# Two layer norms of a decoder trunk: gain and shift applied behind the transposition, as per-partition scalars

## The chip, the core and the metric

The kernel runs on one core of one Trainium2 chip. The metric is the device time of one execution in microseconds (us). PE is the matrix engine, DVE the vector engine, ACT the scalar engine, POOL is GpSimd, SP the engine whose queue issues nearly all DMAs.

## The reference, cut to what matters

```python
def layer_norm(x, g, b):
    xf = x.astype(jnp.float32)
    mu = jnp.mean(xf, -1, keepdims=True)
    var = jnp.mean(jnp.square(xf - mu), -1, keepdims=True)
    return ((xf - mu) * lax.rsqrt(var + LN_EPS) * g + b).astype(x.dtype)

x = layer_norm(x, ln_in_g, ln_in_b)
memn = layer_norm(mem, ln_mem_g, ln_mem_b)
for l in range(DEPTH):
    h = x @ w_in[l]
    ...                                  # two attention groups on slices of h
    x = layer_norm(DEEPNORM_ALPHA * x + mix, ln1_g[l], ln1_b[l])
    xa = memory_cross_attn(x, memn, xa_wq[l], xa_wkv[l], xa_wo[l])
    x = layer_norm(DEEPNORM_ALPHA * x + xa, ln2_g[l], ln2_b[l])
    f = conv_ffn(x, w_up, conv_w, conv_b, w_down)
    x = layer_norm(DEEPNORM_ALPHA * x + f, ln3_g[l], ln3_b[l])
```

x and mem are 256 rows of 1024, all in 32-bit floats; there are two layers. The first norm of x is wanted twice: transposed, for the products with w_in, and in its natural form, for the residual at the end of the first attention block.

## The kernel before

Every large product is taken with split operands: a number is a high part (rounded by ACT, `hi` and `xh`) and a low part (the rest, by a subtraction on DVE, `lo` and `xl`), and three of the four partial products are summed in PSUM. The 256 rows are two tiles of 128 (t = 0, 1), the 1024 columns are 8 chunks of 128 (k = 0 to 7).

Weights stream through `piece` (called by `wmat`): SP loads 512 KB into one of 4 `raw` buffers, ACT makes `hi` (L130), DVE makes `lo` (L131) out of `raw` and `hi`. A `raw` buffer is free when both have read it; the `hi` and `lo` buffers (6 of each) are free when PE has used them. SP issues its loads in a fixed order, so one load that waits for a `raw` buffer holds all behind it. The first pieces are w_kc (2 pieces), then those of the steps nq1, nq0, k (2 each), the compression's w1 (4) and v (3).

The program starts with a few matmuls on ones (`warm`) and with the first norm. Four matmuls of one row of ones (L274) spread gain and shift over 128 partitions in PSUM. `layer_norm` takes the statistics (DVE for t = 0, ACT for t = 1), GpSimd the reciprocal root (L209), and DVE applies mean, gain, root and shift in two passes of two halves (L239, L240). `transposed` then transposes 4 chunks at a time on PE (L247), ACT rounds them into xh (L250), and DVE subtracts into xl (L251). The memory's norm (`mem_norm`) does the same with gain and shift broadcast by DMA (`mg`, 512 KB each).

The steps of a block are named in a list (CFG, 'attn'): kc nq1 nq0 par k cmp v mem tab qk0 ... In `in_kc` (L487) the three partial products come in the order hi·xh, hi·xl, lo·xh. The step tab loads `neg` and lets GpSimd make the bias table alibi, 8 instructions (L323), before the other tables. In `compress` the hidden layer lies in PSUM (cmp); DVE copies it to `hs` (L160), and PE transposes `hs` (L523).

A scheduler gives each engine one fixed order of instructions out of the program, and each engine keeps to it; the row of an instruction is thus also what stands in front of it.

Of the kernel before, what the change touches and what calls it, by code (L numbers as in the profile page):

```python
# [53 lines left out]
def consts():  # L54
# [35 lines left out]
def trunk(ctx: ExitStack, tc: tile.TileContext, a: dict, out: bass.AP):  # L90
# [24 lines left out]
    RAW, HL, PP = SIZES  # L115

    def piece(nk, n, segs, wn=None, cols=None):
        r = wp.tile([P, 1024], F32, name="raw", tag="raw", bufs=RAW)
        rv = r[:, :nk * n].rearrange("p (k n) -> p k n", k=nk)
        for krange, crange, src, *pr in segs:  # L120
            p0, p1 = pr[0] if pr else (0, P)
            nc.sync.dma_start(rv[p0:p1, krange[0]:krange[1], crange[0]:crange[1]], src)
        wn = wn or n
        h = wp.tile([P, 1024], F32R, name="hi", tag="hi", bufs=HL)
        lo = wp.tile([P, 1024], F32R, name="lo", tag="lo", bufs=HL)
        hv = h[:, :nk * wn].rearrange("p (k n) -> p k n", k=nk)
# [53 lines left out]

    xn = [big.tile([P, D], F32, name=f"x{t}", tag=f"x{t}") for t in range(NT)]
    nc.sync.dma_start(xn[0], a["x"][0, 0:P, :])

    def load_gb(g, b, tags=("vmla", "k0")):
        ts_ = []
# [6 lines left out]
    nc.sync.dma_start(xn[1], a["x"][0, P:2 * P, :])
    rows = big.tile([1, 2, D], F32, name="rows", tag="oTh")
    for i, v in enumerate(("ln_in_g", "ln_in_b")):
        nc.scalar.dma_start(rows[:, i], a[v].rearrange("(o d) -> o d", o=1))
    ident = loadc("c_ident", [P, P])
    ones = big.tile([P, 512], F32R, name="ones", tag="q0")
# [10 lines left out]
    def rsqrt(o, x):  # L208
        G.tensor_tensor(o, x, mhalf, op=ALU.pow)  # L209
# [53 lines left out]
    def new_xT():  # L263
# [52 lines left out]
    cok = const.tile([P, NT, HN, 16], F32, name="c_cok", tag="c_cok")  # L316
    alibi = const.tile([P, HN, S], BF16, name="alibi", tag="alibi")

    def load_tables():
        neg = tmp.tile([P, S], F32, name="neg", tag="pT", bufs=4)  # L320
        nc.sync.dma_start(neg, a["c_neg"])
        for h in range(HN):
            G.tensor_scalar(alibi[:, h, :], neg, float(8.0 * 2.0 ** (-(h + 1))), None, op0=ALU.mult)  # L323
        nc.sync.dma_start(tri, a["c_tri"])
        nc.sync.dma_start(cs, a["c_cs"])
        nc.sync.dma_start(kcs, a["c_kcs"])
        nc.sync.dma_start(ctab, a["c_ctab"])
        nc.sync.dma_start(cok, a["c_cok"])
# [2 lines left out]

    def mem_norm():
        mb = big.tile([P, NT, D], F32, name="mb", tag="xkl")
        mg = big.tile([P, 2, D], F32, name="mg", tag="xkh")
        mn, mgb = [mb[:, t] for t in range(NT)], [mg[:, i] for i in range(2)]
        for i, v in enumerate(("ln_mem_g", "ln_mem_b")):
            nc.sync.dma_start(mgb[i], bcast(a[v], D))
# [58 lines left out]
    for l in range(DEPTH):  # L396
# [388 lines left out]
        def mem():  # L785
# [276 lines left out]
```

## Time and profile before

| | us |
|---|---|
| median of 3 runs | 878.4 (877.24 to 880.74) |
| the profiled execution, its own time | 879.98 |
| its span on the core | 877.9 |
| PE busy in the span | 860.3 |
| DVE busy | 665.2 |
| ACT busy | 532.5 |
| GpSimd busy | 132.4 |

Times in the views are counted from the span's start. Each view is one profiled execution. PE's share counts a matmul as busy until its modelled end. A matmul on 256 columns follows the one ahead of it at 0.12 us at the full granted clock.

### The profile page before, as it was taken

What the parts mean: (1) busy time and instruction counts of PE and PEld (TensorE: products, weight loads), DVE (VectorE), ACT (ScalarE), POOL (GpSimd) and SP (SyncE); (2) the same over time, 40 slices, a digit from 0 to 9 for tenths busy, and PEclk for the clock granted to TensorE, in tenths of its full rate; (3) what the DMA queues carried; (4) which work ended last, traced back from release to release, by engine and by line L of the source; (5) the groups of instructions that cost most, each with busy time, mean ns of one, the idle gap of its engine ahead of it and who ended that gap; (6) DMA issues with size and microseconds to landing.
All of it is one profiled execution on the core that took longest, in us unless ns stands there. A gap on an engine that the chain in (4) does not pass through costs nothing.

```text
span 877.9 us, 14948 instructions
## 1 busy us (share of the span) xinstructions
PE 860.3 (98%) x5502; PEld 766.7 (87%) x5502; DVE 665.2 (76%) x1290; ACT 532.5 (61%) x1014; POOL 132.4 (15%) x140
## 2 busy tenths in 40 slices
PE   8989999999999999999999999999999999999996
PEld 5989798899989888888989998879998888888895
DVE  7789887766578877677688788968566877777777
ACT  5658764555546676666555678636573567667661
POOL 1052000000000332222300020000000033223220
PEclk9989999999999999999999999999999999999998
DMA  7944463476347756656538634446633655665641
GB/s 229 284 145 124 132 173 113 140 251 190 96 123 237 217 158 216 190 165 217 183 110 239 190 90 110 144 127 210 194 119 121 218 159 179 212 192 171 215 142 48
DMA packets 128236, 148.66 MB, mean 169 GB/s; under 512 B 6259, under 2 KB 111009, under 8 KB 128163
## 3 DMA queue, kind: packets, MB, share of 16 engines
q1 hardware_dynamic: 128159, 147.70, 54.5%
q8 instruction: 43, 0.70, 0.3%
q14 instruction: 30, 0.25, 0.1%
q10 hardware_dynamic: 4, 0.01, 0.0%
HBM read 146.64 MB, written 1.05 MB: 168 GB/s over the span
## 4 chain that ended last, share of the span: by engine, by line
PE 91%; DVE 4%; ACT 2%; DMA 2%; issue 1%; POOL 0%; SPq 0%; DVEq 0%; ACTq 0%; POOLq 0%
PE up L259 16%; PE up L261 8%; PE acc L996 5%; PE acc L997 5%; PE acc L998 5%; PE acc L170 3%; PE acc L171 3%; PE acc L169 3%; PE fill L178 2%; PE fill L179 2%; PE xq L179 2%; PE xq L178 2%; PE xq L177 2%; PE fill L171 2%; PE fill L169 2%; PE fill L170 2%
## 5 line engine op out<-in xcount | busy, mean ns | idle before, releaser
L131 DVE TENSOR_TENSOR lo<-raw,hi 128x1024 fp32r<-128x1024 f32 (+5 forms) x296 | 322.8, 1108 | 96.2 <-ACT hi L130 94.0
L130 ACT ACTIVATE hi<-raw 128x1024 fp32r<-128x1024 f32 (+5 forms) x296 | 275.8, 951 | 108.9 <-PE acc L171 34.4
L259 PE MATMUL up<-xT,hi 128*128 128x512 f32 x608 | 152.1, 392 | 0.0
L259 PEld LDWEIGHTS up<-xT,hi 128*128 128x128 f32 x608 | 110.3, 189 | 20.3
L261 PEld LDWEIGHTS up<-xT,lo 128*128 128x128 f32 x608 | 82.9, 190 | 5.9
L984 POOL TENSOR_TENSOR cv<-cv 128x256 f32<-128x256 f32 x40 | 54.2, 1356 | 218.7 <-ACT cv L982 170.0
L261 PE MATMUL up<-xT,lo 128*128 128x256 f32 x608 | 84.8, 282 | 0.0
L978 ACT ACTIVATE cv<-u,par 128x256 f32<-128x256 f32 x76 | 45.4, 598 | 49.6 <-DVE u L971 49.6
L996 PE MATMUL acc<-hi,frh 128*128 128x512 f32 x176 | 68.9, 392 | 0.0
L997 PE MATMUL acc<-lo,frh 128*128 128x512 f32 x176 | 68.8, 391 | 0.0
L998 PE MATMUL acc<-hi,frl 128*128 128x512 f32 x176 | 68.2, 389 | 0.0
L209 POOL TENSOR_TENSOR mv<-mv,mhalf 128x1 f32<-128x1 f32 x16 | 14.3, 897 | 309.0 <-DVE mv L233 158.5
L979 DVE SCALAR_TENSOR_TENSOR cv<-u,par,cv 128x255 f32<-128x255 f32 x76 | 37.6, 495 | 26.4 <-ACT cv L978 26.4
L584 ACT ACTIVATE p<-p,nm 128x128 f32<-128x128 f32 x96 | 42.6, 447 | 9.7 <-DVE nm L581 9.4
L986 ACT ACTIVATE frh<-cv 128x256 fp32r<-128x256 f32 x44 | 18.4, 418 | 37.8 <-POOL cv L984 35.4
L987 POOL TENSOR_TENSOR frl<-cv,frh 128x256 fp32r<-128x256 f32 x40 | 38.0, 952 | 20.3 <-ACT frh L986 20.3
L980 DVE SCALAR_TENSOR_TENSOR cv<-u,par,cv 128x254 f32<-128x254 f32 x76 | 37.9, 498 | 2.5
L998 PEld LDWEIGHTS acc<-hi,frl 128*128 128x128 f32 x176 | 33.0, 188 | 7.5 <-DVE frl L987 0.7
L996 PEld LDWEIGHTS acc<-hi,frh 128*128 128x128 f32 x176 | 33.1, 188 | 7.0 <-ACT frh L986 0.9
L997 PEld LDWEIGHTS acc<-lo,frh 128*128 128x128 f32 x176 | 33.1, 188 | 6.0
L177 PE MATMUL fill<-mTh,hi 128*128 128x256 f32 x128 | 37.2, 291 | 0.0
L179 PE MATMUL fill<-mTh,lo 128*128 128x256 f32 x128 | 36.6, 286 | 0.0
(279 smaller groups left out, 2151.7 us busy)
## 6 DMA issues: line engine op xcount, KB each, us to landing
raw<-in_ffn_w_up SPq DMA_DIRECT2D x88, 512.0 KB, 4.4
raw<-in_ffn_w_down SPq DMA_DIRECT2D x44, 512.0 KB, 4.3
raw<-in_xa_wkv SPq DMA_DIRECT2D x32, 512.0 KB, 3.8
raw<-in_xa_wq SPq DMA_DIRECT2D x16, 512.0 KB, 5.4
raw<-in_xa_wo SPq DMA_DIRECT2D x16, 512.0 KB, 4.2
raw<-in_w_in SPq DMA_DIRECT2D x24, 256.0 KB, 3.4
raw<-in_w_out SPq DMA_DIRECT2D x16, 256.0 KB, 4.6
raw<-in_w_out SPq DMA_DIRECT2D x8, 512.0 KB
```

Of the source, the lines that this page charges most:

```text
L130: A.activation(h_, x_, AF.Copy)
L131: V.tensor_tensor(l_, x_, h_.bitcast(F32), op=ALU.subtract)
L169: T.matmul(o, xh_[:, t, k], h, start=k == 0, stop=False)
L177: T.matmul(o, h[:, ms], xh_[:, :, k], start=k == 0, stop=False)
L179: T.matmul(o, lo[:, ms], xh_[:, :, k], start=False, stop=k == len(ws) - 1)
L259: T.matmul(o, h[:, ms], x2[:, k], start=k == 0, stop=False)
L261: T.matmul(o[:, 0:S], lo[:, ms], x2[:, k, 0], start=False, stop=k == len(ws) - 1)
L978: A.activation(c, u, AF.Identity, bias=pcol("cb", l, ft), scale=w_[2])
L984: E.tensor_tensor(conv[0], conv[0], conv[1], op=ALU.mult)
L996: T.matmul(o, fh[:, ts_], h[:, cs_], start=f == 0, stop=False)
L997: T.matmul(o, fh[:, ts_], lo[:, cs_], start=False, stop=False)
L998: T.matmul(o, fl[:, ts_], h[:, cs_], start=False, stop=f == NF - 1)
```

## The change

The broadcast of gain and shift by matmul, and mg with its two broadcast loads, are gone. ACT's queue loads the four vectors as a tile of 32 rows; one transposition makes `gcol`, in which a column holds gain or shift of 128 features. `normalized` takes the statistics on DVE for both tiles and applies mean and root in one pass (L281 of the kernel after). `affine_T` transposes, and then ACT applies gain and shift as scale and bias per partition while it rounds (L293); DVE does the same in two instructions, into y and then xl (L295, L296), one chunk k of both tiles at a time.

The low parts of w_kc are made by GpSimd (`share`; L133), and the table alibi is made by GpSimd from the start on. A new step nx, between par and k, loads gain and shift broadcast (gbx, 2 x 512 KB) and lets GpSimd bring both tiles of x to their natural form in four passes. In `in_kc` the order is hi·xh, lo·xh, hi·xl. In CFG only 'nx' is added.

```diff
+        E = G if share["on"] else V
...
-            V.tensor_tensor(l_, x_, h_.bitcast(F32), op=ALU.subtract)
+            E.tensor_tensor(l_, x_, h_.bitcast(F32), op=ALU.subtract)
...
+    rows = tmp.tile([32, P], F32, name="rows", tag="pT", bufs=4)
+    for i, v in enumerate(("ln_in_g", "ln_in_b", "ln_mem_g", "ln_mem_b")):
+        nc.scalar.dma_start(rows[8 * i:8 * i + 8], a[v].rearrange("(k p) -> k p", p=P))
...
+    def normalized(y):
...
+        for c in range(2):
+            V.bn_stats(s6[:, c, :], y[:, c * 512:(c + 1) * 512])
+        V.bn_aggr(mv[:, 0:2], s6)
+        V.tensor_scalar(mv[:, 2:3], mv[:, 1:2], LN_EPS, None, op0=ALU.add)
+        rsqrt(mv[:, 3:4], mv[:, 2:3])
+        V.tensor_scalar(y, y, mv[:, 0:1], mv[:, 3:4], op0=ALU.subtract, op1=ALU.mult)
+
+    def affine_T(zs, i, h, lo):
...
+                T.transpose(pts[k // 2][:, c0:c0 + P], zs[t][:, k * P:(k + 1) * P], ident)
+        for k in range(KD):
...
+            A.activation(h[:, :, k], src, AF.Identity, scale=g_, bias=b_)
+            y = tmp.tile([P, NT, P], F32, name="y", tag="pp", bufs=PP)
+            V.tensor_scalar(y, src, g_, b_, op0=ALU.mult, op1=ALU.add)
+            V.tensor_tensor(lo[:, :, k], y, h[:, :, k].bitcast(F32), op=ALU.subtract)
...
-    gb = []
-    for i in range(2):
-        gb.append([bank("fill") for _ in range(2)])
-        for c in range(2):
-            T.matmul(gb[i][c], ones[0:1, 0:P].bitcast(F32), rows[:, i, c * 512:(c + 1) * 512], start=True, stop=True)
+    pg = bank("fill")
+    T.transpose(pg[:, 0:32], rows, ident[0:32, 0:32])
+    V.tensor_copy(gcol.rearrange("p a k -> p (a k)"), pg[:, 0:32])
+    warm(12, 512)
     xh, xl = new_xT()
     for t in range(NT):
-        layer_norm(xn[t], gb, act=cfg['lnact']['in'][t])
-        if t:
-            warm(6, 512)
-        transposed(xn[t], t, xh, xl)
-
+        normalized(xn[t])
+    share["on"] = True
     w_kc = wmat(a["w_in"][0], [(C_KC, C_KC + 256)])
+    share["on"] = False
+    affine_T(xn, 0, xh, xl)
+
+    def natural_x():
+        gb = big.tile([P, 2, D], F32, name="gbx", tag="oTh")
+        for i, v in enumerate(("ln_in_g", "ln_in_b")):
+            nc.sync.dma_start(gb[:, i], bcast(a[v], D))
+            for t in range(NT):
+                G.tensor_tensor(xn[t], xn[t], gb[:, i], op=(ALU.mult, ALU.add)[i])
...
+    neg = tmp.tile([P, S], F32, name="neg", tag="pT", bufs=4)
+    nc.sync.dma_start(neg, a["c_neg"])
+    for h in range(HN):
+        G.tensor_scalar(alibi[:, h, :], neg, float(8.0 * 2.0 ** (-(h + 1))), None, op0=ALU.mult)
+
     def load_tables():
-        neg = tmp.tile([P, S], F32, name="neg", tag="pT", bufs=4)
-        nc.sync.dma_start(neg, a["c_neg"])
-        for h in range(HN):
-            G.tensor_scalar(alibi[:, h, :], neg, float(8.0 * 2.0 ** (-(h + 1))), None, op0=ALU.mult)
...
         for t in range(NT):
-            layer_norm(mn[t], mgb, act=cfg['lnact']['mem'][t])
-            transposed(mn[t], t, mh, ml)
+            normalized(mb[:, t])
+        affine_T([mb[:, t] for t in range(NT)], 1, mh, ml)
...
-                        T.matmul(pbs[j], w_[i == 2][:, j * P:(j + 1) * P], (xl if i == 1 else xh)[:, :, k],
+                        T.matmul(pbs[j], w_[i == 1][:, j * P:(j + 1) * P], (xl if i == 2 else xh)[:, :, k],
```

GpSimd's order from the first reciprocal root on, before (mv: the norms' statistics, ss: those of a later norm):

```order
L209 TENSOR_TENSOR mv_104<-mv_104,mhalf_84 128x1
L209 TENSOR_TENSOR mv_129<-mv_129,mhalf_84 128x1
L323 TENSOR_SCALAR alibi_179<-neg_744 128x256 x8
L209 TENSOR_TENSOR mv_716<-mv_716,mhalf_84 128x1
L209 TENSOR_TENSOR mv_691<-mv_691,mhalf_84 128x1
```

and after (lo_134 and lo_140: the low parts of w_kc; x0, x1: the tiles of x):

```order
L212 TENSOR_TENSOR mv_115<-mv_115,mhalf_87 128x1
L212 TENSOR_TENSOR mv_123<-mv_123,mhalf_87 128x1
L357 TENSOR_SCALAR alibi_201<-neg_202 128x256 x2
L133 TENSOR_TENSOR lo_134<-raw_131,hi_133 128x1024
L357 TENSOR_SCALAR alibi_201<-neg_202 128x256
L133 TENSOR_TENSOR lo_140<-raw_137,hi_139 128x1024
L357 TENSOR_SCALAR alibi_201<-neg_202 128x256 x5
L316 TENSOR_TENSOR x0_73<-x0_73,gbx_446 128x1024
L316 TENSOR_TENSOR x1_74<-x1_74,gbx_446 128x1024
L316 TENSOR_TENSOR x0_73<-x0_73,gbx_446 128x1024
L316 TENSOR_TENSOR x1_74<-x1_74,gbx_446 128x1024
L212 TENSOR_TENSOR mv_727<-mv_727,mhalf_87 128x1
```

The two low parts of w_kc stand behind two and three of the table's instructions, and the four passes on x stand between the table and the memory's first root.

ACT's order where x's transposed chunks are read out of PSUM, before (hi_265 and hi_274 are nq1's pieces, hi_336 nq0's first):

```order
L130 ACTIVATE hi_265<-raw_262 128x4x128 x2
L250 ACTIVATE xT_103<-lnt_115 128x4x128
L130 ACTIVATE hi_274<-raw_271 128x4x128
L250 ACTIVATE xT_103<-lnt_122 128x4x128
L130 ACTIVATE hi_274<-raw_271 128x4x128
L130 ACTIVATE hi_336<-raw_333 128x4x128 x2
L250 ACTIVATE xT_103<-lnt_147 128x4x128
L250 ACTIVATE xT_103<-lnt_154 128x4x128
```

and after (lnt_143 holds the chunks 0 and 1, lnt_144 2 and 3, lnt_145 4 and 5, lnt_146 6 and 7; hi_368 and hi_377 are nq0's pieces):

```order
L293 ACTIVATE xT_114<-lnt_145,gcol_84 128x256
L293 ACTIVATE xT_114<-lnt_143,gcol_84 128x256
L293 ACTIVATE xT_114<-lnt_146,gcol_84 128x256
L132 ACTIVATE hi_306<-raw_303 128x4x128 x2
L293 ACTIVATE xT_114<-lnt_144,gcol_84 128x256
L132 ACTIVATE hi_368<-raw_365 128x4x128 x2
L132 ACTIVATE hi_377<-raw_374 128x4x128
L293 ACTIVATE xT_114<-lnt_145,gcol_84 128x256
L132 ACTIVATE hi_377<-raw_374 128x4x128
L293 ACTIVATE xT_114<-lnt_146,gcol_84 128x256
```

The chunks 5 and 7 of x now stand behind the halves of nq0's second piece, raw_374. With 4 raw buffers, raw_365 takes over the buffer of raw_131, and raw_374 that of raw_137; these are the two that GpSimd's lo_134 and lo_140 read.

## Rows read from the trace of the kernel before

**Rows 1.** The page's head: the span and the busy time of each engine.

```profile
span 877.9 us, 14948 instructions
PE 860.3 (98%) x5502; PEld 766.7 (87%) x5502; DVE 665.2 (76%) x1290; ACT 532.5 (61%) x1014; POOL 132.4 (15%) x140
```

**Rows 2.** Waits of PE, 0 to 120 us: total, times, longest us.

```profile
PE cmp L523 <- DVE hs L160: 3.2, 1, 3.2
PE pt L597 <- ACT pT L600: 0.9, 2, 0.6
```

**Rows 3.** Stretches: us, busy (instructions) of PE, PEld, DVE, ACT, POOL; PE's clock; DMA share, GB/s.

```profile
17.46:34.84 17.38, 17.38 (x145) 17.38 (x145) 14.51 (x25) 9.48 (x18) 0.00 (x0) 1.00 0.95 262
34.84:46.40 11.56, 11.56 (x100) 11.56 (x99) 7.70 (x14) 6.63 (x9) 1.31 (x2) 1.00 0.98 296
47.58:50.77 3.19, 0.01 (x2) 0.01 (x1) 3.10 (x6) 2.61 (x5) 3.19 (x4) 0.82 0.86 260
50.77:56.46 5.69, 5.69 (x26) 5.62 (x27) 5.69 (x17) 3.46 (x9) 5.44 (x5) 0.50 0.72 212
```

**Rows 4.** Timeline of DVE around the copy hs: start, duration, line, idle before.

```profile
40.63 1.03 DVE L131 TENSOR_TENSOR lo<-raw,hi 128x840 fp32r<-128x840 f32 x1 [0.24 <-ACT hi L130]
...
44.61 0.69 DVE L220 BATCH_NORM_STATS2 s<-mb 128x6 f32<-128x512 f32 x1 [2.95 <-DMA mb<-in_mem]
45.22 1.09 DVE L131 TENSOR_TENSOR lo<-raw,hi 128x840 fp32r<-128x840 f32 x1
...
50.03 0.68 DVE L160 COPY hs<-cmp 34x512 f32<-34x512 f32 x1
```

**Rows 5.** Timeline of PE at the start.

```profile
11.41 1.97 PE L247 MATMUL lnt<-c_ident,x 128*128 128x128 f32 x8 [0.77 <-DVE x L240]
13.03 2.76 PE L203 MATMUL lnt<-ones 128*128 128x512 f32 x6
16.14 1.33 PE L247 MATMUL lnt<-c_ident,x 128*128 128x128 f32 x8 [0.35 <-issue]
```

**Rows 6.** GpSimd by source line: count, duration in ns (min/median/max), first and last start.

```profile
L323 POOL TENSOR_SCALAR alibi<-neg x8: 846/1000/2482, 45.0 to 54.2; 128x256 bf16<-128x256 f32 x8
L435 POOL TENSOR_TENSOR kr<-m x4: 252/332/700, 81.8 to 520.5; 128x32 f32<-128x32 f32 x4
L987 POOL TENSOR_TENSOR frl<-cv,frh x40: 733/834/1488, 285.3 to 849.8; 128x256 fp32r<-128x256 f32 x40
```

**Rows 7.** Timelines of GpSimd and of DVE, 290 to 291.5 us.

```profile
290.43 0.74 POOL L984 TENSOR_TENSOR cv<-cv 128x256 f32<-128x256 f32 x1 [3.68 <-ACT cv L982]
...
290.60 0.85 DVE L980 SCALAR_TENSOR_TENSOR cv<-u,par,cv 128x254 f32<-128x254 f32 x1
```

**Rows 8.** Timeline of ACT at the start.

```profile
11.72 1.15 ACT L130 ACTIVATE hi<-raw 128x512 fp32r<-128x512 f32 x2 [0.21 <-DMA raw<-in_w_in]
...
13.55 0.63 ACT L130 ACTIVATE hi<-raw 128x512 fp32r<-128x512 f32 x1 [0.19 <-DMA raw<-in_w_in]
```

**Rows 9.** SP's queue: timeline, then DMA issues (x, KB each, us to landing).

```profile
17.89 4.52 SPq L122 DMA_DIRECT2D raw<-in_w_in  x6
...
38.07 0.65 SPq L339 DMA_DIRECT2D mb<-in_mem  x1
...
mg<-in_ln_mem_g SPq DMA_DIRECT2D x1, 512.0 KB, 3.7
mb<-in_mem SPq DMA_DIRECT2D x2, 512.0 KB, 6.5
```

**Rows 10.** DVE and ACT on 256 columns: by line (busy us, mean ns), and by source (ns).

```profile
L154 DVE TENSOR_SCALAR p<-p,sm 128x256 f32<-128x256 f32 x48 | 16.6, 345 | 0.0
L978 ACT ACTIVATE cv<-up,par 128x256 f32<-128x256 f32 x12 | 6.5, 559 | 4.4 <-PE up L179 2.5 <-DVE cv L980 1.9
...
L154 DVE TENSOR_SCALAR cqn<-proj,ss x4: 470/550/617, 516.6 to 535.0; 128x256 f32<-128x256 f32 x2, 128x384 f32<-128x384 f32 x2
L987 DVE TENSOR_TENSOR frl<-cv,frh x4: 425/426/426, 445.5 to 862.2; 128x256 fp32r<-128x256 f32 x4
```

More of the change, by code (lines that the diff above doesn't have):

```diff
@@ L81 @@
 CFG = [
-    {'attn': 'kc nq1 nq0 par k cmp v mem tab qk0 cq qk1 cps ckv cmt fill av0 qk2 av1 av2 ch qk3 kr mq2 mq0 fill mkv par2 mq1 mq3 av3 mqk2 mqk3 mqk0 mqk1 mav0 mav1 fill mav3 mav2', 'cross': 'q2 q3 q0 q1 qk2 qk3 qk0 v0 v2 v1 qk1 av2 av0 v3 av1 av3', 'ev': [[[0, 0], [1, 0]], [1, 1]], 'fill': 2, 'lnfill': 3, 'vord': (1, 0, 3, 2), 'xt': ('q1', 'k1', 'q0'), 'opt': {'B': 0, 'M': 1, 'C': 0, 'N00': 0, 'N01': 0, 'N10': 0, 'N11': 0, 'N20': 0, 'N21': 0, 'R0': 1, 'R1': 1, 'K': 0, 'H': 0, 'X0': 0, 'X1': 1}, 'lnact': {'in': [0, 1], 'mem': [1, 0], '1': [1, 1], '2': [0, 0], '3': [0, 1]}, 'last': 5, 'natural': 0, 'bank': {'acc0': 'a', 'acc1': 'a', 'fill': 'a', 'proj': 'a', 'pv': 'a', 'mpv': 'b', 'mlav': 'b', 'xpv': 'b', 'nat': 'a', 'lnt': 'b', 'par': 'a', 'projt': 'a', 'cmp': 'b', 'cmps': 'b', 'cmpt': 'a', 'pt': 'b', 'qk': 'b', 'cht': 'a', 'mla': 'a', 'mqk': 'b', 'xq': 'a', 'xqk': 'a', 'xpt': 'b', 'up': 'b'}},
+    {'attn': 'kc nq1 nq0 par nx k cmp v mem tab qk0 cq qk1 cps ckv cmt fill av0 qk2 av1 av2 ch qk3 kr mq2 mq0 fill mkv par2 mq1 mq3 av3 mqk2 mqk3 mqk0 mqk1 mav0 mav1 fill mav3 mav2', 'cross': 'q2 q3 q0 q1 qk2 qk3 qk0 v0 v2 v1 qk1 av2 av0 v3 av1 av3', 'ev': [[[0, 0], [1, 0]], [1, 1]], 'fill': 2, 'lnfill': 3, 'vord': (1, 0, 3, 2), 'xt': ('q1', 'k1', 'q0'), 'opt': {'B': 0, 'M': 1, 'C': 0, 'N00': 0, 'N01': 0, 'N10': 0, 'N11': 0, 'N20': 0, 'N21': 0, 'R0': 1, 'R1': 1, 'K': 0, 'H': 0, 'X0': 0, 'X1': 1}, 'lnact': {'in': [0, 1], 'mem': [1, 0], '1': [1, 1], '2': [0, 0], '3': [0, 1]}, 'last': 5, 'natural': 0, 'bank': {'acc0': 'a', 'acc1': 'a', 'fill': 'a', 'proj': 'a', 'pv': 'a', 'mpv': 'b', 'mlav': 'b', 'xpv': 'b', 'nat': 'a', 'lnt': 'b', 'par': 'a', 'projt': 'a', 'cmp': 'b', 'cmps': 'b', 'cmpt': 'a', 'pt': 'b', 'qk': 'b', 'cht': 'a', 'mla': 'a', 'mqk': 'b', 'xq': 'a', 'xqk': 'a', 'xpt': 'b', 'up': 'b'}},
@@ L115, in trunk @@
     RAW, HL, PP = SIZES
+    share = {"on": False}
     def piece(nk, n, segs, wn=None, cols=None):
@@ L182, in trunk @@
     nc.sync.dma_start(xn[0], a["x"][0, 0:P, :])
+    nc.sync.dma_start(xn[1], a["x"][0, P:2 * P, :])
     def load_gb(g, b, tags=("vmla", "k0")):
@@ L190, in load_gb @@
         return ts_
[L192 to L195, printed above, removed]
     ident = loadc("c_ident", [P, P])
+    rows = tmp.tile([32, P], F32, name="rows", tag="pT", bufs=4)
+    for i, v in enumerate(("ln_in_g", "ln_in_b", "ln_mem_g", "ln_mem_b")):
+        nc.scalar.dma_start(rows[8 * i:8 * i + 8], a[v].rearrange("(k p) -> k p", p=P))
+    gcol = const.tile([P, 4, KD], F32, name="gcol", tag="gcol")
     ones = big.tile([P, 512], F32R, name="ones", tag="q0")
@@ L267, in new_xT @@
         return [v[:, 0], v[:, 1]]
-    warm(8, 256)
-    gb = []
-    for i in range(2):
-        gb.append([bank("fill") for _ in range(2)])
-        for c in range(2):
-            T.matmul(gb[i][c], ones[0:1, 0:P].bitcast(F32), rows[:, i, c * 512:(c + 1) * 512], start=True, stop=True)
+    def normalized(y):
+        mv = st.tile([P, 6], F32, name="mv", tag="mv")
+        s6 = st.tile([P, 2, 6], F32, name="s6", tag="s6")
+        for c in range(2):
[4 more added lines that the diff above has]
+        V.tensor_scalar(y, y, mv[:, 0:1], mv[:, 3:4], op0=ALU.subtract, op1=ALU.mult)
@@ new lines, in affine_T @@
+    def affine_T(zs, i, h, lo):
+        pts = [bank("lnt") for _ in range(4)]
+        for t in range(NT):
+            for k in range(KD):
+                c0 = (k % 2) * S + t * P
+                T.transpose(pts[k // 2][:, c0:c0 + P], zs[t][:, k * P:(k + 1) * P], ident)
+        for k in range(KD):
+            src = pts[k // 2][:, (k % 2) * S:(k % 2 + 1) * S].rearrange("p (t n) -> p t n", t=NT)
+            g_, b_ = gcol[:, 2 * i, k:k + 1], gcol[:, 2 * i + 1, k:k + 1]
+            A.activation(h[:, :, k], src, AF.Identity, scale=g_, bias=b_)
+            y = tmp.tile([P, NT, P], F32, name="y", tag="pp", bufs=PP)
+            V.tensor_scalar(y, src, g_, b_, op0=ALU.mult, op1=ALU.add)
+            V.tensor_tensor(lo[:, :, k], y, h[:, :, k].bitcast(F32), op=ALU.subtract)
@@ L283, in trunk @@
+    def natural_x():
+        gb = big.tile([P, 2, D], F32, name="gbx", tag="oTh")
+        for i, v in enumerate(("ln_in_g", "ln_in_b")):
+            nc.sync.dma_start(gb[:, i], bcast(a[v], D))
+            for t in range(NT):
+                G.tensor_tensor(xn[t], xn[t], gb[:, i], op=(ALU.mult, ALU.add)[i])
     par = const.tile([P, NPAR], F32, name="par", tag="par")
@@ L333, in mem_norm @@
         mb = big.tile([P, NT, D], F32, name="mb", tag="xkl")
[L334 to L337, printed above, removed]
         for t in range(NT):
-            nc.sync.dma_start(mn[t], a["mem"][0, t * P:(t + 1) * P, :])
+            nc.sync.dma_start(mb[:, t], a["mem"][0, t * P:(t + 1) * P, :])
         for t in range(NT):
-            layer_norm(mn[t], mgb, act=cfg['lnact']['mem'][t])
-            transposed(mn[t], t, mh, ml)
+            normalized(mb[:, t])
+        affine_T([mb[:, t] for t in range(NT)], 1, mh, ml)
     class KV:
@@ L797, in trunk @@
             "tab": load_tables,
+            "nx": natural_x,
             "cmp": lambda: e.update(vct=compress(e["c2"])),
```

## The prediction

> **What bounds the kernel now.** I read the page's head first: PE is busy for 860.3 of 877.9 us [rows 1], so a change outside PE is worth only what it takes out of PE's idle time or out of time at the low clock. Next PE's waits in the first 120 us, where everything lies that the change touches [rows 2]: the reader is to see one wait that matters, 3.2 us of the transposition of hs for DVE's copy. The stretches [rows 3] show what it really costs: PE stands still from 47.58 to 50.77, and from 50.77 to 56.46 the granted clock is 0.50 (1.2 instead of 2.4 GHz), so another 5.69/2 = 2.85 us is lost, 6.0 us together. DVE's timeline [rows 4] shows why: DVE waited 2.95 us for the memory's rows (mb) with its statistics, and the low parts queued behind went one after another until hs at 50.03, 5.42 us after the landing. The second place is the start: PE's first real product begins at 17.46, and from there to 46.40 it never waits [rows 3]. So there are two prizes: up to about 3.7 us at the start (first chunk of x at 13.8 instead, below) and up to 6.0 us at hs.
>
> **The change part by part.** The sum is against the profiled execution, 879.98 us with a span of 877.9; it lies 1.6 above the median of 878.4, so I take the difference and add it to the median.
>
> *Removed.* The broadcast matmuls, two of DVE's passes over x and ACT's statistics all lie ahead of 17.46, and so does the one transposition for gcol. PE has x's two tiles transposed by 12 instead of 17.5, but that is not what is late next.
>
> *GpSimd's low parts.* A two-input instruction takes 0.25 us on 32 columns and 0.73 on 256 [rows 6], 2.2 ns a column, so an estimated 2.4 us on 1024. neg is loaded ahead of nq1's pieces; ACT got these at 11.72 and 13.55 [rows 8], 1.83 us per 512 KB, so the 128 KB of neg land at about 10.3 and delay the pieces by 0.45. Two alibi instructions at 0.85 [rows 6] end at 12.0, lo_134 ends at 14.4. DVE wants its own two subtractions for nq1 by then. In the trace a two-input GpSimd instruction at 290.43 made the DVE instruction of 290.60, with two inputs on 254 columns, take 0.85 where one on 256 takes 0.43 alone [rows 7, 10], and alibi instructions took up to 2.48 beside DVE's subtractions [rows 6]: the two engines take turns. So DVE's 2 x 0.6 go first at 14.4, the third alibi ends near 16.4, and lo_140 at 18.8 (without any turns 17.6).
>
> *What waits for it.* raw_365 and raw_374 take the buffers that lo_134 and lo_140 read, and all of SP's queue stands behind them. raw_374 is issued at 18.8; 512 KB on idle DMA engines took 3.7 us to land [rows 9], so 22.5. Before, six issues of the same row of loads began at 17.89 [rows 9]. ACT has chunk 5 of x behind raw_374's first half: 0.6 for the half and 0.56 for the chunk [rows 10], done at 23.6 (bounds 21.5 and 24.5). DVE's own pairs per chunk, 0.47 and 0.43 [rows 10], do not come later than that.
>
> *PE.* It starts kc at 13.8 (ACT: nq1's first piece 12.15 to 13.3, then chunk 0), but its order holds only 24 of the 144 matmuls of kc, nq1 and nq0 ahead of chunk 5. The other 120 at 0.12 (17.38 us for 145, [rows 3]) take 14.4 us from 23.6: 38.0 at the full clock. From 13.8 to 23.6 PE has 3 to 5 us of work, and in the trace it fell to half clock after a standstill of 3.19 us and came back after 5.69 us of work, at the start between 11.41 and 16.14 (transpositions of 0.25 each first, of 0.17 later), so within 4.7 us [rows 3, 5]. So I let it work its first 4 to 5.7 us at half clock, which loses 2.0 to 2.85, and take 2.4. nq0 ends at 40.4 instead of 34.84, **5.6 us late** (bounds 2.5 and 6.5).
>
> *Then hs.* k and the first layer of the compression, 11.56 us [rows 3], bring PE to 52.0, and 11 matmuls of v, now ahead of hs instead of 8, to 53.4. The high and low buffers of w1 come free with nq0, so the low parts and, behind them, the load of mb's second half (38.07 before, [rows 9]) shift by about 5. On top come GpSimd's four passes over x, 4 x 2.4 = 9.6 us between 26 and 39, in turns with DVE's low parts of k and w1; I count 0.8 + 1.6 + 2.2 = 4.6 us that DVE stands, none if DVE always comes first. mb is thus issued between 42.6 and 45.8 and lands 3.7 to 6.5 us later [rows 9], between 46.3 and 52; I take 49.3, DVE being the later chain. From there to hs DVE has the 5.42 us of before [rows 4] plus one more statistics instruction (0.6), its aggregation (0.2) and a pass on 1024 columns (0.35 for 256, [rows 10]; about 0.65): 6.9, with hs 0.7, so PE goes on at **56.9** (bounds 53.9 and 59.6). It went on at 50.77, with 3 matmuls (0.4 us) fewer done. The standstill of 3.5 us is as long as before, so the half clock behind it costs the same. Difference: 56.9 - 50.77 - 0.4 = +5.7.
>
> *Elsewhere at nothing.* gbx's 1 MB replaces mg's 1 MB on the same queue. Behind hs DVE loses 12 instructions on 512 columns, 0.69 for one of that size [rows 4], 8.3 us, and gains 8 pairs of 0.9, so about 1 us less, ACT the like; PE waits there only 0.9 us more in all [rows 2], so +-1 us. Alibi leaves a place where nobody waited for it. The natural form of x is read 90 us later.
>
> One rule speaks to the size. What the trace shows first: alibi's first instruction, from 45.03, overlapped DVE's subtraction of 45.22, which took 1.09 [rows 4], against 1.03 for one of the same size without company, and so barely cost DVE anything. The Trainium skill ("SBUF — State Buffer", section "SBUF: two separate sides") says that the port pair of GpSimd and VectorE is an exclusive lock, held for a whole instruction by whichever starts first. For the two-input case the trace agrees (0.85 against 0.43), for alibi it does not; by the rule the six alibi instructions behind lo_134 would also stop DVE for up to 6 x 0.85 = 5.1 us, and the sum would be nearer +10.
>
> Sum: +5.7, rounded down to **+5.5** for the 0.9 us of waits behind that may vanish: 878.4 + 5.5 = 883.9 us, 0.6% slower.
>
> **The rivals.**
> (a) *The late start is swallowed at hs.* The 6.0 us lost there are a reserve: if DVE's low parts come ahead of GpSimd's passes and mb lands by 46.5, hs is ready at 53.9 when PE has just come (53.4), and no low clock follows. Then PE goes on at 53.9 at full speed; before, 50.77 at half clock is worth 50.77 + 2.85 = 53.6: difference 53.9 - 0.4 - 53.6 = -0.1, and with the bounds of the late start -3 to +2: 875.4 to 880.4. For it: DMA is less crowded once SP is held up. Against: four instructions of 2.4 us on the engine that DVE takes turns with.
> (b) *Faster.* raw_374 is not held up: GpSimd's instruction on 1024 columns takes no more than DVE's 1.2, and lo_140 ends by 15. Then chunk 5 is there at about 18.5, PE works from 13.8 with short gaps and keeps its clock, nq0 ends at 31 to 33 (-2 to -4), and hs is swallowed as in (a) (-3 to -4 more): about -6, 872. It decides from lo_140's end at 15.5 on. Against: 2.2 ns a column twice over [rows 6].
> (c) *Worse.* Any GpSimd instruction stops DVE while it runs, alibi too; x's low chunks and later mb come another 3 to 5 us late: +8 to +13, 886 to 891. The 45.22 instruction speaks against it.
>
> **How the numbers follow.** The forecast has 0.45 (+2 to +8, 880.4 to 886.4), (a) 0.32, (b) 0.12, (c) 0.11. The likeliest is 883.9. The range leaves out (b) and the upper two thirds of (c), which makes 0.2: 875.4 to 888. Half a per cent is 4.4 us, about what a measurement of this kernel can tell from no change: faster by more is (b), 0.12; slower by more is (c) and 0.35 of the forecast, 0.46; the rest, (a) and the forecast's lower end, is 0.42. Cases of both signs hold chance; the forecast's own range is 880.4 to 886.4.
>
> **What the profile after would show.** Right: GpSimd's two instructions on w_kc at 2.4 us or more, SP's seventh load of a weight at 18 to 20 us, ACT idle for it ahead of chunk 5, PE with under half its time busy between 14 and 23 and a clock of 0.50 behind it, and PE waiting for hs near 53 to 57. Wrong: lo_140 done by 16; PE without a wait over 1 us between 14 and 25; hs ready when PE comes; or a wait of more than 1 us between 60 and 130 that was not there.

## The result and the profile after

The kernel after takes 893.52 us, median of 4 runs (892.7 to 894.91), against 878.86 (877.24 to 880.74) of the kernel before on the same chip: a ratio of 1.0168, interval [1.0147, 1.0189], or 14.7 us slower. The forecast was 883.9, with a range of 875.4 to 888.0. So the sign of the likeliest case held, and the size did not. The profiled execution has a span of 892.4 us, 14.5 more than before [rows 1]:

```profile
span 892.4 us, 14964 instructions
PE 862.7 (97%) x5501; PEld 770.7 (86%) x5501; DVE 678.6 (76%) x1305; ACT 532.0 (60%) x1014; POOL 146.4 (16%) x146
```

PE is busy 2.4 us more (time at the half clock counts as busy) and idle 12 us more. Its five largest waits up to 130 us, where there was one of 3.2 before [rows 2] (columns: who waited, for whom; total, times, longest us; cmp L555 is the transposition of hs):

```profile
PE projt L180 <- DVE xT L296: 3.8, 1, 3.8
PE par L339 <- issue: 3.5, 1, 3.5
PE cmp L555 <- DVE mv L279: 2.4, 1, 2.4
PE projt L519 <- ACT xT L293: 2.1, 1, 2.1
PE qk L648 <- ACT pT L632: 1.5, 1, 1.5
```

By the start of matching matmuls in both traces, PE is 3.9 us late at the end of nq0, 10.6 at the transposition of hs, 8.7 at 74 us, 10.9 at 95 us and 14.7 from 115 us on; the last value stays to the end. So there are three steps: about 4, about 7, and about 4 us (6 from the low point at 74 us).

**The first step.** GpSimd's timeline (start, duration, line, count, idle before), and under it DVE's:

```profile
10.24 1.87 POOL L357 TENSOR_SCALAR alibi<-neg 128x256 bf16<-128x256 f32 x2 [0.60 <-DMA neg<-in_c_neg]
12.08 2.36 POOL L133 TENSOR_TENSOR lo<-raw,hi 128x1024 fp32r<-128x1024 f32 x1
14.40 1.29 POOL L357 TENSOR_SCALAR alibi<-neg 128x256 bf16<-128x256 f32 x1
15.67 2.34 POOL L133 TENSOR_TENSOR lo<-raw,hi 128x1024 fp32r<-128x1024 f32 x1
17.98 4.74 POOL L357 TENSOR_SCALAR alibi<-neg 128x256 bf16<-128x256 f32 x5
25.42 10.83 POOL L316 TENSOR_TENSOR x<-x,gbx 128x1024 f32<-128x1024 f32 x4 [2.70 <-DMA gbx<-in_ln_in_g]
```

```profile
12.72 3.06 DVE L133 TENSOR_TENSOR lo<-raw,hi 128x512 fp32r<-128x512 f32 x2 [2.24 <-ACT hi L132]
15.71 0.53 DVE L295 TENSOR_SCALAR y<-lnt,gcol 128x256 f32<-128x256 f32 x1
16.28 2.01 DVE L296 TENSOR_TENSOR xT<-y,xT 128x256 fp32r<-128x256 f32 x1
...
25.15 0.68 DVE L133 TENSOR_TENSOR lo<-raw,hi 128x512 fp32r<-128x512 f32 x1
25.75 2.62 DVE L296 TENSOR_TENSOR xT<-y,xT 128x256 fp32r<-128x256 f32 x1
28.30 8.50 DVE L133 TENSOR_TENSOR lo<-raw,hi 128x512 fp32r<-128x512 f32 x3
36.72 0.27 DVE L530 TENSOR_TENSOR c2l<-projt,c2h 64x128 fp32r<-64x128 f32 x1
```

The two low parts of w_kc take 2.36 and 2.34 us. The two DVE subtractions of 12.72, some 1.4 us of work, take 3.06 beside lo_134; the first chunk's subtraction of 16.28, 0.42 without company, ends at 18.29, just behind lo_140 (18.01). PE, which started kc at 13.72, waits 3.8 us for it, until 18.34, and then works at the half clock, with no wait until one of 0.4 at 28.4, again for a subtraction:

```profile
14.00:20.00 6.00, 2.17 (x10) 1.88 (x10) 5.96 (x9) 3.40 (x8) 6.00 (x6) 0.50 0.46 121
20.00:30.00 10.00, 9.56 (x63) 9.25 (x63) 10.00 (x14) 3.89 (x8) 7.18 (x5) 0.79 0.89 244
```

(columns as in rows 3: the stretch, its length, busy time of PE, PEld, DVE, ACT and POOL, granted clock, DMA share, GB/s.)

**The second step.** Between 25.75 and 36.72 DVE finishes four subtractions, one for each of GpSimd's four passes on x. The view of lo (count, least/median/most ns, first and last start) has the low parts of this stretch at a median of 2882 ns, where the undisturbed one takes 683:

```profile
L133 DVE TENSOR_TENSOR lo<-raw,hi x5: 683/2882/2890, 25.1 to 36.9; 128x512 fp32r<-128x512 f32 x4, 128x1024 fp32r<-128x1024 f32 x1
```

DVE thus stands for 8.7 of 11 us. What follows: the subtractions c2l, which free PSUM banks, start at 36.72 (22.86 before). The loads of the compression's w1 go out from 31.25 (22.70 before). PE stands 3.5 us ahead of the transposition of par at 42.41 (the view names no releaser; a subtraction c2l has ended 0.1 us earlier) and 1.3 us ahead of k, and the clock is 0.50 from 44 to 48. The memory's second half is loaded at 48.12 instead of 38.07 [rows 9], and hs is copied at 60.65 instead of 50.03 [rows 4]:

```profile
48.12 0.47 SPq L371 DMA_DIRECT2D mb<-in_mem  x1
```

```profile
60.65 0.68 DVE L162 COPY hs<-cmp 34x512 f32<-34x512 f32 x1
```

**The third step** lies between 74 and 115 us. DVE has the memory's 8 pairs (L295 and L296, one pair for each chunk) from 71.5 to 80.3 and comes to its first softmax instruction 13.0 us later than before; before, then after:

```profile
66.74 0.28 DVE L581 CUSTOM_DVE_ANT_0 p<-qk,alibi 128x128 f32<-128x128 f32 x1
```

```profile
79.69 0.28 DVE L613 CUSTOM_DVE_ANT_0 p<-qk,alibi 128x128 f32<-128x128 f32 x1
```

PE then has five waits between 90 and 116 us, 3.1 us together, for the softmax's DVE and ACT work, and 6.8 us at the half clock (columns as above):

```profile
95.91:102.74 6.83, 6.29 (x25) 5.17 (x26) 6.45 (x29) 3.78 (x15) 1.53 (x4) 0.50 0.23 52
```

That the pairs are what makes DVE late here is argued from its order, not shown.

### The profile page after: what moved, and what is told of

It is laid out like the page before. It is cut to its first block, busy times and chain, and to the rows that moved or that the text cites. A ratio compares the mean times of both kernels' runs of the same rounds, so it can differ in the third digit from the quotient of the medians.

```text
span 892.4 us, 14964 instructions
## 1 busy us (share of the span) xinstructions
PE 862.7 (97%) x5501; PEld 770.7 (86%) x5501; DVE 678.6 (76%) x1305; ACT 532.0 (60%) x1014; POOL 146.4 (16%) x146
## 4 chain that ended last, share of the span: by engine, by line
PE 89%; DVE 6%; DMA 2%; issue 1%; ACT 1%; SPq 0%; ACTq 0%; DVEq 0%; POOL 0%
PE up L262 16%; PE up L264 8%; PE acc L1029 5%; PE acc L1030 5%; PE acc L1031 4%; PE acc L172 3%; PE acc L173 3%; PE acc L171 3%; DVE lo L133 2%; PE fill L180 2%; PE fill L181 2%; PE fill L179 2%; PE fill L173 2%; PE xq L181 2%; PE xq L180 2%; PE xq L179 2%
## 5 line engine op out<-in xcount | busy, mean ns | idle before, releaser
L133 DVE TENSOR_TENSOR lo<-raw,hi 128x1024 fp32r<-128x1024 f32 (+5 forms) x294 | 329.7, 1137 | 100.2 <-ACT hi L132 97.7
L180 PE MATMUL fill<-mTl,hi 128*128 128x256 f32 x128 | 37.3, 291 | 0.0
```

The source lines that it names most:

```text
L133: E.tensor_tensor(l_, x_, h_.bitcast(F32), op=ALU.subtract)
L180: T.matmul(o, h[:, ms], xl_[:, :, k], start=False, stop=False)
```

## The experiments

Each set of runs had the kernel before beside it (878.9 to 880.6 us); ratios and "us behind" are against that, so that the kernel after is 14.7 behind. Two theories at first. A (turns): a GpSimd instruction with two inputs from SBUF and DVE's two-input subtractions exclude each other for the whole instruction. B (late loads): what is late comes from raw_365 and raw_374 and from what stands behind them in SP's queue.

**e1_lo_dve**

```diff
-    share["on"] = True
+    share["on"] = False
```

> The kernel after with one part undone: the low parts of w_kc are made by DVE again. Theory A (turns: a GpSimd instruction with two inputs from SBUF on 1024 columns keeps DVE's two-input subtractions waiting for all of its 2.3 to 2.7 us): without lo_134 and lo_140 DVE's first pair for x is done by 15 instead of 18.3, raw_374 is no longer held up, and nq0 ends at 34 to 36 instead of 38.9. But the four passes on x still hold DVE behind it, so that only part of it comes through: 888 to 892 us against 893.5. Theory B (the late loads behind raw_365 and raw_374 are what costs, all the way down to the memory's rows; GpSimd's passes are hidden): 884 to 888.

Measured 889.53 us, ratio 1.0124 [1.0109, 1.0139]: 10.3 behind, 4.3 less than the kernel after. That is theory A's range, but nq0 ended at 38.6, not at 34 to 36. The trace shows why: the passes now began at 20.71 and held a low part (2.38 us), the last chunk's subtraction (2.56 us) and two of three further low parts (6.25 us for the three). All of this lay some 4 us earlier than in the kernel after (c2l from 32.88 on instead of 36.72).

**e2_no_passes**

```diff
             nc.sync.dma_start(gb[:, i], bcast(a[v], D))
-            for t in range(NT):
-                G.tensor_tensor(xn[t], xn[t], gb[:, i], op=(ALU.mult, ALU.add)[i])
```

> The kernel after without GpSimd's four passes on x; the loads of gbx stay, and so does the order of every other instruction. It leaves out gain and shift of x's natural form. Theory A (turns): DVE's three low parts between 28.3 and 36.8 take 2 us instead of 8.5, hs comes 6 to 9 us earlier, and the time is 881 to 887 us. Theory B (late loads): the passes lie beside work that waits for loads anyway; 892 to 894.

Measured 889.58 us, 1.0123 [1.0106, 1.0139]: 10.4 behind, 4.3 less than the kernel after, neither theory's number. The order of every other instruction is that of the kernel after, on each engine. DVE's timeline has the effect that A names, 1.89 instead of 8.50:

```profile
25.85 0.42 DVE L296 TENSOR_TENSOR xT<-y,xT 128x256 fp32r<-128x256 f32 x1
26.18 1.89 DVE L133 TENSOR_TENSOR lo<-raw,hi 128x512 fp32r<-128x512 f32 x3
```

PE's standstill between nq0 and k, 4.8 us in the kernel after, shrank to 1.2. But hs came only 4.4 us earlier (56.21). With the passes gone DVE waited 2.24, 1.10 and 0.73 us for ACT's high parts behind it, and ACT before them for loads (1.46 and 1.31 us for w_in). So of 8.7 us saved on DVE half came through. Both theories have a share.

**e4_one_input**

```diff
-                G.tensor_tensor(xn[t], xn[t], gb[:, i], op=(ALU.mult, ALU.add)[i])
+                G.tensor_scalar(xn[t], xn[t], (0.999, 1.001)[i], None, op0=ALU.mult)
```

> The kernel after with GpSimd's four passes on x as instructions with one input (a multiplication by a constant, 128x1024, 32 bits, in place), in the same order on every engine. It leaves out gain and shift of x's natural form. If the turns come from two inputs alone (the table's one-input instructions between 18.0 and 22.7 let DVE go on in the trace): within 2 us of the kernel without the passes. If any GpSimd instruction of this size keeps DVE's two-input subtractions waiting: DVE's three low parts still take over 6 us, and the time is above it by two thirds or more of what the passes cost.

Measured 889.92 us, 1.0124 [1.0106, 1.0141]: as without the passes, again with every engine's order kept. GpSimd is as busy as in the kernel after, and DVE goes on (GpSimd's row, then DVE's):

```profile
22.79 11.59 POOL L316 TENSOR_SCALAR x<-x 128x1024 f32<-128x1024 f32 x4
```

```profile
26.08 2.73 DVE L133 TENSOR_TENSOR lo<-raw,hi 128x512 fp32r<-128x512 f32 x3
...
30.12 1.23 DVE L133 TENSOR_TENSOR lo<-raw,hi 128x1024 fp32r<-128x1024 f32 x1 [1.11 <-ACT hi L132]
```

It is the second input that makes the engines take turns here, not the length and not GpSimd's being busy.

**e3_passes_dve**

```diff
-                G.tensor_tensor(xn[t], xn[t], gb[:, i], op=(ALU.mult, ALU.add)[i])
+                V.tensor_tensor(xn[t], xn[t], gb[:, i], op=(ALU.mult, ALU.add)[i])
```

> The kernel after with the four passes on x made by DVE instead of GpSimd. Theory A (turns): DVE works 4 x 1.2 = 4.9 us on them, instead of standing for 8.7; 888 to 891 us. Theory B (late loads; DVE has room there): as after, 892 to 895, since DVE's own work grows and no load comes earlier. A third way, that the passes cost DVE nothing on GpSimd but 4.9 on DVE itself, gives 896 to 899.

Measured 887.56 us, 1.0098 [1.0083, 1.0113]: 8.4 behind, 6.3 less than the kernel after. The same work costs less on the busy engine (four passes of 1.2 us) than on the idle one. It came out below even e2_no_passes; the order of DVE and SP had changed with it (both halves of mb are issued at 32.15 there, ahead of v's pieces), so that difference isn't the passes' alone.

**e6_before_passes**, the step nx alone (the passes and the loads of gbx), in the kernel before:

```diff
-kc nq1 nq0 par k cmp
+kc nq1 nq0 par nx k cmp
```

> The kernel before with one part of the change alone: the step nx (loads of gbx and GpSimd's four passes on x) behind par. Gain and shift are thus taken twice in x's natural form. Theory A (turns): DVE is 80% busy with low parts from 20 to 40 us, each pass of 2.4 to 2.7 us holds it, hs comes 4 to 8 us later, and the time is 882 to 887 us against 879.5. Theory B (the passes only hurt where loads are already late): 879 to 881.

Measured 889.96 us, 1.0108 [1.0085, 1.0132]: 9.4 us slower than the kernel before, more than theory A's range, and clear of B's number. The two engines' rows show the same picture on DVE without any other part of the change:

```profile
17.61 10.81 POOL L288 TENSOR_TENSOR x<-x,gbx 128x1024 f32<-128x1024 f32 x4 [5.21 <-DVE lo L131]
```

```profile
18.67 11.51 DVE L131 TENSOR_TENSOR lo<-raw,hi 128x512 fp32r<-128x512 f32 x6
```

Six low parts of some 0.7 take 11.5 us; four of them were held, one for each pass. But the 9.4 us are not the price of these turns alone. Here gbx's 1 MB comes on top of mg's, while the DMA engines were busy 0.95 and 0.98 of the time in the kernel before [rows 3], and PE, DVE and ACT got another order behind it. PE waits for DVE in six places between 26 and 69 us, yet at 57 us it is only 0.5 us late, since the clock stays at 1.00 behind hs. The largest wait, 3.4 us, comes after that, and GpSimd's queue stands behind it: neg lands late, the memory's root follows the table, and DVE waits for the root:

```profile
51.50 7.49 POOL L330 TENSOR_SCALAR alibi<-neg 128x256 bf16<-128x256 f32 x8 [23.07 <-DMA neg<-in_c_neg]
59.07 0.56 POOL L209 TENSOR_TENSOR mv<-mv,mhalf 128x1 f32<-128x1 f32 x1
```

```profile
59.67 0.75 DVE L240 SCALAR_TENSOR_TENSOR mb<-mb,mv,mg 128x512 f32<-128x512 f32 x1 [3.16 <-POOL mv L209]
```

No run has the loads of gbx alone in this kernel.

**e8_lo_dve_passes_dve** (e1 and e3 together)

> The kernel after with both two-input jobs taken from GpSimd: the low parts of w_kc and the four passes on x are DVE's. If the two prices add (4.0 and 5.9 us measured one by one): 882 to 885. If the start's delay is hidden behind the same wait for hs: 886 to 888. The memory's norm stays as in the kernel after, so by theory C a wait of 3 us or more remains for PE between 85 and 98.

Measured 884.03 us, 1.0056 [1.0039, 1.0072]: the two prices add (4.3 + 6.3, measured 10.2). PE is on time at the end of nq0 (0.3 us late). So taking the two-input work from GpSimd, with the new order that this gave the engines, is worth two thirds of the loss, and 4.5 us remain. PE waits 2.5 us between 85 and 98 us, where theory C had 3 or more.

**e5_mem_old** and **e9_x_only** (e8 with the same edit): the memory's norm as before.

```diff
...
-            normalized(mb[:, t])
-        affine_T([mb[:, t] for t in range(NT)], 1, mh, ml)
+            layer_norm(mn[t], mgb, act=cfg['lnact']['mem'][t])
+            transposed(mn[t], t, mh, ml)
...
```

> The kernel after with the memory's norm as before: statistics on DVE and ACT, gain and shift from mg in the natural form, transposition of four chunks and one subtraction for four. Theory C (DVE works off the memory's norm ahead of hs and ahead of the first softmax, and its 8 pairs wait for both tiles; that is the step of about 4 us that PE loses between 90 and 98 us, and 2 to 3 us at hs): 886 to 890. Theory D (PE's loss between 90 and 98 only passes on how late DVE is from GpSimd's passes and the late loads): 892 to 895.

> As the run before, and the memory's norm as before the change: of the change there remain x's own norm (columns' scalars), the table early on GpSimd, and the four passes on DVE. If the three parts (two-input work on GpSimd, its passes, the memory's norm) are the whole loss: 874 to 880. If columns' scalars for x are themselves dear (8 pairs of 0.9 instead of 4 subtractions of 0.7 on DVE at the start): 880 to 884.

Measured 893.98 us (1.0164 [1.0141, 1.0186]) and 883.61 (1.0044 [1.0027, 1.0061]): no gain beyond the noise either time (0.3 and 0.4 us), where theory C had 886 to 890 for the first. In e5_mem_old PE has one wait between 84 and 98 us, of 1.2, but waits 0.6 and 1.2 us for pT behind 105, and the median is as late as that of the kernel after. e9's number is one that its expectation gave to a dear new form of x's norm; e17 and e21 below speak against that. With several causes on top of one another, undoing one showed nothing.

**e10_x_only_late**, **e13_late_warm**, **e14_warm_nx_end**, **e19_spread_dve**: what eats the early start, and where DVE has room for the passes. They build on e9_x_only; in e14 the passes stand behind par2 and in e19 between av1 and av3.

```diff
-kc nq1 nq0 par nx k ... cps ckv cmt fill av0
+kc nq1 nq0 par k ... cps ckv cmt nx fill av0
```

> As the run before, with the step nx moved from behind par to behind cmt, so that DVE's four passes on x (4.9 us) lie behind the copy hs. If DVE's queue ahead of hs is what PE waits for: 2 to 5 us below the run before, 870 to 877. If the passes hit DVE as hard at the later place: the same within 1.5 us.

```diff
+        if i == 0:
+            pw = bank("fill")
+            for r in range(16):
+                T.transpose(pw[:, (r % 4) * P:(r % 4 + 1) * P], zs[1][:, (r % 8) * P:(r % 8 + 1) * P], ident)
```

> The run e10_x_only_late with 16 more transpositions of x (into a bank that nobody reads) behind those that are wanted, so that PE stands no longer from 11.6 to 13.8 us. In that run the products from 13.8 to 20.6 ran at the half clock (0.21 us for one of 256 columns instead of 0.12). If the clock is what eats the early start: 2 to 3 us below it, 880 to 881.5. If x's chunks, one each 1.2 us of DVE's pairs, are what PE waits for: PE waits 2 to 3 us more between 14 and 23 and the time is within 1 us of it, 882.5 to 884.

Measured 883.29 us (1.0044 [1.0031, 1.0058]) and 882.31 (1.0028 [1.0010, 1.0046]). The first moved nothing: PE was 2.0 us ahead of the kernel before at 77 us, and lost 4 by 87 us, where the passes now lay in front of the softmax (without them, in e17_warm_no_passes below, it lost none there). The second gained 1 to 2 at most, not 2 to 3; the two intervals overlap. PE's waits from 13 to 24 us and the stretch from 14 to 21, of e10_x_only_late:

```profile
PE projt L523 <- ACT xT L293: 3.1, 2, 2.3
14.00:21.00 7.00, 6.17 (x29) 5.88 (x30) 6.86 (x15) 5.62 (x12) 6.82 (x6) 0.52 0.69 187
```

and of e13_late_warm:

```profile
PE projt L527 <- ACT xT L297: 2.0, 2, 1.4
PE projt L180 <- DVE xT L300: 1.3, 3, 0.7
14.00:21.00 7.00, 4.64 (x32) 3.93 (x31) 6.86 (x16) 5.45 (x13) 6.63 (x6) 1.00 0.68 182
```

At the full clock PE does a little more work (32 matmuls against 29) in 4.64 us instead of 6.17 and waits instead: DVE is busy 6.86 of 7 us in both, with 8 pairs for x and the low parts between them. By 34 us PE is level with the kernel before in both (0.2 and 0.1 us late). So the rate at which DVE hands over the chunks, not the clock, sets when nq0 is through, and the kernel before, with 4 subtractions there, is no later. Starting kc at 13.8 instead of 17.46 is worth nothing here.

```diff
-        gb = big.tile([P, 2, D], F32, name="gbx", tag="oTh")
...
+        for c in range(0, D, 256):
+            for i, v in enumerate(("ln_in_g", "ln_in_b")):
+                gb = tmp.tile([P, 256], F32, name="gbx", tag="pT", bufs=4)
...
```

> As the run before, with the passes on x's natural form in 16 pieces of 256 columns on DVE, behind par2 (about 105 to 140 us), where PE waits for nobody. In e10_x_only_late PE was 2.0 us ahead of the kernel before at 77 us and lost 4 between 77 and 87, where three of DVE's four passes stood. If these passes are the cause: 876 to 879. If DVE, 90% busy behind 105 us, hands the passes on to PE there: 881 to 884.

> The run e13_late_warm with the passes on x's natural form in eight pieces of 512 columns (0.7 us each on DVE), in four steps between av1 and av3, from about 88 us on. If three passes of 1.2 us between 68 and 82 us were the cause there: 877 to 880. If DVE has no room anywhere behind hs: 881 to 884.

Measured 881.71 us (1.0014 [0.9997, 1.0030]) and 885.23 (1.0058 [1.0035, 1.0081]). Behind par2 no gain is clear of the noise (in the profiled execution, a late one of 882.98, PE is ahead by 2.3 at 82 us and behind by 3.5 from 162 us on); spread from av1 to av3 the median is 3.6 further behind, at the edge of the noise. DVE has no free place for them between 68 and 160 us that these runs found.

**e15_after_warm**, the same transpositions in the kernel after:

> The kernel after with the same 16 transpositions more. There PE waits 3.8 us until 18.3 for DVE's first pair, which stands behind GpSimd's low part of w_kc. If that wait alone lets the clock fall: no gain, 892 to 894. If the gap ahead of the first product does: 889 to 891.

Measured 892.79 us, 1.0145 [1.0121, 1.0169]. The interval overlaps that of the kernel after: no gain beyond the noise. DVE's first pair is held by GpSimd as before (2.02 us for the subtraction of 16.05), PE waits 4.2 us between 10 and 30 us, and the clock is at 0.50 from 15.6 to 25.8.

**e17_warm_no_passes**, **e18_lo_dve_no_passes** and **e21_no_passes_mem_old**: e13 and e8 without the passes, and e18 with the memory's norm as before.

> The run e13_late_warm without the four passes on x's natural form (the loads stay). It leaves out gain and shift there. If the passes cost the last 4 us: PE keeps the 3 to 4 us by which it was ahead at 65 us, 876 to 879 against 882.3. If x's columns' form itself does: 881 to 883.

> The kernel after with the low parts of w_kc on DVE and without the four passes on x (loads stay), the memory's norm as in the kernel after. It leaves out gain and shift of x's natural form. If the passes on DVE cost the last 4 us: 879 to 881 against 884.0. If not: 883 to 885, and x's columns' form or the memory's norm keeps the rest.

> The run e18_lo_dve_no_passes with the memory's norm as in the kernel before. It leaves out gain and shift of x's natural form. If the memory's 8 pairs are what PE loses between 82 and 90 us: 878 to 880 against 883.1. If the loss stays or moves on to 100 to 110 us, as in e5_mem_old: 882 to 884.

Measured 878.56 us (0.9989 [0.9974, 1.0003]), 883.05 (1.0032 [1.0017, 1.0047]) and 880.41 (1.0004 [0.9993, 1.0016]). With the passes and the memory's new norm gone (e17, e21) the kernel is level with the one before: applying gain and shift behind the transposition for x, and making the table early, are by themselves worth nothing either way. Under the memory's new norm leaving the passes out gives only 1.3 (e18 against e8); under the old one it gives 3.1 (e17 against e13) and 3.5 (e21 against e9). PE's waits from 60 to 130 us of e18_lo_dve_no_passes, and of e17_warm_no_passes:

```profile
PE qk L646 <- ACT pT L630: 1.5, 1, 1.5
PE cmpt L705 <- DVE pc L698: 0.8, 1, 0.8
PE pt L627 <- DVE nm L611: 0.6, 1, 0.6
PE pt L627 <- DVE pT L632: 0.6, 1, 0.6
PE qk L665 <- ACT pT L630: 0.5, 1, 0.5
```

```profile
PE cmpt L713 <- DVE pc L706: 1.0, 1, 1.0
PE pt L635 <- ACT pT L638: 0.3, 1, 0.3
```

In e18 PE is on time at 77 us (0.3 late). DVE has the memory's 8 pairs from 62.2 to 70.9 and comes to the first softmax at 70.28, 3.5 us later than before (66.74).

The account, in us behind the kernel before: 14.7 = 10.2 (GpSimd's two-input work, down to 4.5 in e8) + 4.0 (the passes once DVE has them, and the memory's norm, down to 0.5 in e21) + 0.5. How the 4.0 divide is not shown: by e18 it is 1.3 for the passes and 2.6 for the norm, by e9 0.4 for the norm and 3.5 for the passes. Each kernel's distance has an interval of 1.0 to 1.5 us either way, so the 10.2 and the 4.0 are clear of the noise and the 0.5 is not. The 10.2 also hold the new order that the scheduler gave e8; with every order kept, the passes alone cost 4.3 (e2), and their second input 3.9 (e4). No version that computes the whole reference beat the kernel before; e14_warm_nx_end came level with it.

## Why the prediction went wrong, by its own steps

- *GpSimd's low parts:* right. 2.4 us each were estimated, 2.36 and 2.34 measured; lo_134 was to end at 14.4 (14.44) and lo_140 at 18.8 (18.01).
- *What waits for it:* right in its times, wrong in who waits. Chunk 5 was to be ready at 23.6 (22.95), and the loads behind raw_374 went out at 19. But PE never waited for chunk 5. It waited 3.8 us for DVE's first subtraction for x, held by lo_134 and lo_140, where the prediction let DVE's pairs come no later than ACT's chunk.
- *PE at the start:* kc began at 13.72 (13.8 forecast), with the half clock behind it, and nq0 was 3.9 us late (5.6, bounds 2.5 and 6.5). That the size is near is in part luck, since another wait made it. The clock stayed at 0.50 from 14.0 to 24.2, with PE busy for 6.4 us of that, where the prediction gave it 4 to 5.7. And it did not fall behind the standstill of 3.19 us in the trace of before, as the prediction reads it, but inside: the mean there is 0.82 [rows 3].
- *GpSimd's four passes:* the step that failed. They were priced at "0.8 + 1.6 + 2.2 = 4.6 us that DVE stands", as if DVE lost a part of each. DVE stood 8.7 us. It had nothing but two-input subtractions queued, so each one waited for a whole pass, and one got in between two passes. The row was at hand: the DVE instruction of 290.60 ended 0.28 us behind GpSimd's [rows 7], so its 0.85 for 0.43 [rows 10] can be read as a wait for the rest of one whole GpSimd instruction, and the turns, not an overlap, were the thing to multiply.
- *Between nq0 and hs:* failed with it. The prediction let k start as soon as PE was free; the banks, freed by c2l behind the held low parts, made PE stand 4.8 us there (1.2 without the passes, in e2), at half clock afterwards. PE went on behind hs at 61.39, past the upper bound of 59.6: 10.6 us late, where +5.7 was forecast.
- *Elsewhere at nothing, +-1:* failed, by about 4 us. It counted DVE's work on the memory's norm (about equal, and so it is) and not when it may begin: 8 pairs wait for both tiles, and the first softmax stands behind them on DVE. How much of the 4 us this makes stays open: undoing the norm gained nothing in the kernel after (e5), and 2.6 only once the passes were gone too (e21 against e18).
- *The sum.* Of the 9.2 us that the forecast lacked, 4.9 lie at hs and 4.1 behind it. One of its signs of being wrong came: a new wait of over 1 us between 60 and 130 us (1.5, behind 90).
- *Rivals.* (a) and (b) did not happen. (c) had the nearest size (886 to 891, below the measured 893.5), though not its mechanism: it let the table's instructions stop DVE too, and they did not (five of them from 17.98 to 22.72, beside DVE subtractions of x that took 0.4 to 0.6).

The sentence from the Trainium skill ("SBUF — State Buffer", section "SBUF: two separate sides") on an exclusive lock, held for a whole instruction by whichever of GpSimd and VectorE starts first, gave a sum "nearer +10", because of the table. The runs agree with it for GpSimd instructions with two inputs (e6_before_passes: 11.5 us for six low parts) and disagree for those with one (e4_one_input: 2.73 us for three beside 11.59 of GpSimd's, 1.89 without); there the measurement decides.

## What to carry to other kernels

Before giving GpSimd work "because it is idle", look at what the vector engine has queued beside it: two-input instructions on both sides took turns at full length here, so 10.8 us of such work on GpSimd cost DVE nearly 9, where DVE itself needs 4.9 for it. An earlier start of PE is worth only what its suppliers can feed: compare the rate of chunks with the rate of matmuls, then the start. And when undoing one part shows nothing, undo it again where the other losses are gone: the memory's norm gave 0.3 and 0.4 us at first, and 2.6 once the passes were gone too. What a part is worth then depends on the order in which the parts are undone; only their sum is measured.

## What was not expected of the hardware

A one-input GpSimd instruction (128x1024, 32 bits, SBUF to SBUF) takes as long as one with two (2.9 against 2.7 us beside DVE's work, four each), but hardly holds DVE's two-input subtractions. And two kinds of DVE instruction ran undisturbed during a two-input GpSimd one. One with a single input, in PSUM: 0.53 us at 15.71 in the kernel after, inside 15.67 to 18.01, while the one with two inputs in SBUF behind it took 2.01. And one with two inputs of which one is in PSUM: in e6_before_passes the second of these two, from 18.07 on, took 0.68 us inside GpSimd's first pass (17.61 to 20.02).

```profile
17.47 1.28 DVE L251 TENSOR_TENSOR xT<-lnt,xT 128x512 fp32r<-128x512 f32 x2
```
